# The first decode of a routed expert layer and four expert blocks, issued in a written order

## The chip, the cores and the metric

The kernel runs on one core of one Trainium2 chip. The core has a matrix engine (TensorE, PE in the profile; its weight loads are PEld), a vector engine (VectorE, DVE), an activation engine (ScalarE, ACT), GpSimd (POOL) and a queue engine that issues most transfers (SyncE, SP). The metric is the device time of one execution in microseconds; lower is better. The time before is the median of 3 runs, 2264.26 us (2261.86 to 2264.97).

## The reference, cut to what matters

Two transformer blocks on 512 tokens of width 1024, in 32-bit floats. The edit lies in the first block's expert layer:

```python
q = (xc @ w_query).reshape(c, PEER_HEADS, 2, D_HALF)
sc = jnp.einsum('chpd,hpkd->chpk', q, sub_keys)
sv, si = lax.top_k(sc, PEER_TOPK)
cand = (sv[:, :, 0, :, None] + sv[:, :, 1, None, :]).reshape(c, PEER_HEADS, PEER_TOPK * PEER_TOPK)
...
fv, fi = lax.top_k(cand, PEER_TOPK)
idx = jnp.take_along_axis(cidx, fi, axis=-1)
g = jax.nn.softmax(fv, axis=-1)
a = jax.nn.gelu(jnp.einsum('chkd,cd->chk', u_tab[idx], xc))
return jnp.einsum('chk,chkd->cd', g * a, v_tab[idx])
```

Each token has 8 heads; each head scores two sets of 128 keys, keeps 16 of each, and chooses 16 pairs. A pair names one of 128 x 128 = 16384 experts, each of which has a row in `u_tab` and a row in `v_tab`.

## The kernel before, in words

The 512 tokens are four tiles of 128. For tile 0 the chosen rows are gathered by GpSimd (`gather_steps`). For tiles 1 to 3 all 16384 experts are computed densely: for each of 128 blocks of 128 experts, the activations of 384 tokens (`h_block`) are multiplied by a gate matrix that is zero where an expert was not chosen, and then by the block's rows of `v_experts`.

A product of 32-bit numbers is made of three matmuls: a weight is loaded (`wload`, line 127, load in line 130), ScalarE makes its high half (`whi`, line 132), VectorE its low half (`wlo`, line 134), and `mm3` (lines 138 to 140) multiplies. Weight tiles have three raw buffers and four for each half. One `h_block` is such a load of 512 KB, 24 matmuls into `hps` (two buffers), and a Gelu on ScalarE (line 488) that evicts it.

Of the 128 dense blocks, 68 are computed ahead of the dense loop and stored to DRAM: `park_blocks` (line 493 is the store) is a generator, and `spread(parks, n)` emits the next n of them. These parked blocks depend on nothing but the normalised input. They are emitted at these places: one in each of the 16 steps of the routing loop, two in each of the four decodes (one ahead of each of its two halves), some in each gate group (`PARKS`), and what is left behind the last group.

The routing loop scores the keys and picks the best 16. `decode(t)` (lines 578 to 627) turns the picked places of tile t into indices and softmax gates: for each of two halves it compares, multiplies and adds 128x2048 elements on VectorE (lines 598 to 605); then come the Exp on ScalarE (line 610), three transposes on TensorE (line 622) and two copies, `sT` and `nT`. `gate_matrix(t, q, ...)` (lines 629 to 656) makes 16 tokens' part of the gate matrix: one-hot rows on VectorE and ScalarE, matmuls (line 650), an eviction (line 652), and a store to `wdr` (line 653). There are 8 groups in each of three tiles. The dense loop reads `wdr` back as `wt` (line 708) and multiplies it with the activations (line 723) before its accumulating matmuls (`acc`). A part of `wt` holds all 24 groups, so it needs the last of them.

A planner orders the instructions of each engine by their place in the text and by what is ready, within the buffers there are. Inside `with tc.manual_schedule():` each engine issues the region's instructions in the order of the text; where other instructions fall among them stays the planner's. Before the change only the dense loop stands in such a region.

Of the kernel before, what the change touches and what calls it, by code (L numbers as in the profile page):

```python
# [43 lines left out]
def body(ctx: ExitStack, tc: tile.TileContext, A: dict, out: bass.AP):  # L44
# [407 lines left out]
    with exp as st:  # L452
# [38 lines left out]
        def park_blocks():  # L491
            for k, n in enumerate(PARKED):
                SY.dma_start(park[k], h_block(n))
                yield
# [22 lines left out]
        parks = park_blocks()  # L517
        gathers = gather_steps()

        def spread(gen, n):  # L520
            for _ in range(n):
                next(gen, None)

        with mix as s1:
# [53 lines left out]
            def decode(t):  # L578
                sif = rt.tile([128, 16, 16], BF16, name="sif", bufs=2)
                V.tensor_copy(sif, si[:, t])  # L580
                fif = fi[:, t].rearrange("p h s -> p (h s)")
                over = rt.tile([128, 128], U32, name="over")
                V.tensor_scalar(over, fif, 64.0, -64.0, op0=OP.max, op1=OP.add)
                V.tensor_scalar(over, over, 2, None, op0=OP.logical_shift_right)
                V.scalar_tensor_tensor(fif, over, 12.0, fif, op0=OP.mult, op1=OP.add)
                sel = []
                for w in range(2):
                    spread(parks, 1)
                    ab = rt.tile([128, 128], U32, name=f"ab{w}")
                    if w == 0:  # L590
                        V.tensor_scalar(ab, fif, 4, None, op0=OP.logical_shift_right)
                    else:
                        V.tensor_scalar(ab, fif, 15, None, op0=OP.bitwise_and)
                    abf = rt.tile([128, 128], F32, name=f"abf{w}")
                    V.tensor_copy(abf, ab)
                    eq = rt.tile([128, 8, 16, 16], BF16, name="eq", bufs=2)
                    eqf = eq.rearrange("p h s a -> p (h s) a")
                    V.tensor_tensor(eqf, abf[:, :, None].to_broadcast([128, 128, 16]),
                                    io[:, None, 0:16].to_broadcast([128, 128, 16]), op=OP.is_equal)
                    src = sif.rearrange("p (h w) a -> p h w a", w=2)[:, :, w, None, :].to_broadcast([128, 8, 16, 16])  # L600
                    V.tensor_tensor(eq, eq, src, op=OP.mult)
                    for half in (8, 4, 2):
                        V.tensor_tensor(eqf[:, :, 0:half], eqf[:, :, 0:half], eqf[:, :, half:2 * half], op=OP.add)
                    sl_ = rt.tile([128, 128], F32, name=f"sel{w}")
                    V.tensor_tensor(sl_, eqf[:, :, 0], eqf[:, :, 1], op=OP.add)
                    sel.append(sl_)
                gw = gw0 if t == 0 else rt.tile([128, 128], F32, name="gw")
                g3 = gw.rearrange("p (h s) -> p h s", h=8)
                V.tensor_tensor(g3, fv[:, t], fv[:, t, :, 0:1].to_broadcast([128, 8, 16]), op=OP.subtract)
                SC.activation(gw, gw, AF.Exp)  # L610
                gs = sm.tile([128, 8], F32, name="gs")
                V.tensor_reduce(gs, g3, axis=AX.X, op=OP.add)
                V.reciprocal(gs, gs)
                V.tensor_tensor(g3, g3, gs[:, :, None].to_broadcast([128, 8, 16]), op=OP.mult)
                if t == 0:
                    ixf = rt.tile([128, 128], F32, name="ixf")
                    V.scalar_tensor_tensor(ixf, sel[0], 128.0, sel[1], op0=OP.mult, op1=OP.add)
                    V.tensor_copy(ix, ixf)
                    return None
                tp = psw.tile([128, 4, 128], F32, name="wps", tag="wps")  # L620
                for k, y in enumerate((sel[0], sel[1], gw)):
                    PE.transpose(tp[:, k, :], y, ident)
                sT = rt.tile([128, 3, 128], F32, name="sT", bufs=2)
                SC.activation(sT, tp[:, 0:3, :], AF.Copy)
                nT = rt.tile([128, 3, 128], F32, name="nT", bufs=2)
                SC.activation(nT, tp[:, 0:3, :], AF.Copy, scale=-1.0)
                return sT, nT
# [29 lines left out]

            quick.close()
            rw = s1.enter_context(tc.tile_pool(name="rw", bufs=2, reuse_waits="tile"))
            ahead = {1: decode(1)}  # L660
            for t in range(1, NT):
                for q in range(128 // TG):
                    if (t, q) in DECODE:
# [474 lines left out]
```

## Time and profile before

| | |
|---|---|
| median of 3 runs | 2264.26 us |
| profiled execution, its own time | 2265.66 us |
| its span, first to last instruction | 2263.9 us |
| mean granted TensorE clock | 0.995 |
| PE busy | 2213.2 us, 98% |
| DVE busy | 1518.0 us, 67% |
| ACT busy | 1012.2 us, 45% |

Busy times are of one profiled execution. A matmul that waits for an operand can count as busy, and shares over the whole span are means over stages with different limits, so the stage around the edit is read by itself. A granted clock of 1.0 is 2.4 GHz, one of 0.5 is 1.2 GHz; a figure between them is a mean over both.

### The profile page before, as it was taken

How to read it: one execution, taken by the hardware profiler on the slowest of the kernel's cores; microseconds unless marked ns; L12 is line 12 of the kernel's file. 1: busy time of each engine (PE TensorE's matmuls, PEld its weight loads, DVE VectorE, ACT ScalarE, POOL GpSimd, SP SyncE). 2: the span in 40 equal slices, each digit the busy share in tenths (PEclk: the TensorE clock that was granted, in tenths of full speed). 3: DMA queues.
4: the chain of work that ended last, by engine and by line, in shares of the span. 5: the costliest groups of instructions: out<-in, count | busy, mean ns of one | idle time of the engine just before them, and what ended most of it. 6: DMA issues, size and time to landing. Idle time of an engine off the chain costs nothing.

```text
span 2263.9 us, 30294 instructions
## 1 busy us (share of the span) xinstructions
PE 2213.2 (98%) x11337; PEld 1917.0 (85%) x11337; DVE 1518.0 (67%) x3026; ACT 1012.2 (45%) x1667; POOL 355.0 (16%) x261
## 2 busy tenths in 40 slices
PE   7999999999899999999999999999999999999998
PEld 6788878888899999888888888888866778888887
DVE  5663467899999985777777777777774667333322
ACT  5475244334996773333333333333353365222222
POOL 0000000000132422333333333333200000000000
PEclk9999999999999999999999999999999999999999
DMA  4203253443697998989989888998732124333332
GB/s 160 92 29 122 84 184 110 129 120 107 241 332 282 368 333 279 318 299 317 323 303 330 298 307 300 331 321 307 259 106 69 55 88 154 93 93 102 94 96 72
DMA packets 179875, 453.21 MB, mean 200 GB/s; under 512 B 15504, under 2 KB 84496, under 8 KB 176656
## 3 DMA queue, kind: packets, MB, share of 16 engines
q1 hardware_dynamic: 142864, 317.04, 41.7%
q0 software_dynamic: 36864, 134.23, 16.8%
q8 instruction: 89, 1.46, 0.3%
q14 instruction: 58, 0.48, 0.1%
HBM read 410.58 MB, written 40.63 MB: 199 GB/s over the span
## 4 chain that ended last, share of the span: by engine, by line
PE 83%; DVE 6%; ACT 4%; issue 4%; DMA 2%; POOL 0%; SPq 0%; DVEq 0%; ACTq 0%; POOLq 0%
PE mm L139 12%; PE mm L138 12%; PE mm L140 12%; PE acc L138 7%; PE acc L140 7%; PE acc L139 7%; PE hps L140 6%; PE hps L138 6%; PE hps L139 6%; PE wps L650 2%; ACT stg L652 1%; PE pv L372 1%; DVE wlo L134 1%; PE sc L928 1%; DVE hres L513 1%
## 5 line engine op out<-in xcount | busy, mean ns | idle before, releaser
L132 ACT ACTIVATE whi<-wraw 128x1024 fp32r<-128x1024 f32 x248 | 258.3, 1047 | 521.5 <-PE mm L139 308.2
L134 DVE TENSOR_TENSOR wlo<-wraw,whi 128x1024 fp32r<-128x1024 f32 x248 | 298.3, 1207 | 258.2 <-ACT whi L132 254.2
L138 PE MATMUL hps<-x2h,whi 128*128 128x384 f32 x1024 | 348.0, 340 | 2.1 <-ACT whi L132 1.8
L140 PE MATMUL hps<-x2h,wlo 128*128 128x384 f32 x1024 | 344.9, 337 | 1.6 <-DVE wlo L134 0.9
L139 PE MATMUL hps<-x2l,whi 128*128 128x384 f32 x1024 | 343.7, 336 | 0.0
L502 POOL DMA_INDIRECT gu<-in_u_experts_dram,ix x128 | 176.1, 1376 | 890.1 <-DVE og L644 579.6
L138 PE MATMUL acc<-whi,hh 128*128 128x512 f32 x768 | 301.8, 393 | 9.4 <-ACT hh L119 9.4
L140 PE MATMUL acc<-whi,hl 128*128 128x512 f32 x768 | 301.9, 393 | 1.1 <-DVE hl L120 1.1
L139 PE MATMUL acc<-wlo,hh 128*128 128x512 f32 x768 | 300.9, 392 | 0.0
L702 DVE TENSOR_TENSOR wlo<-wraw,whi 128x1024 fp32r<-128x1024 f32 x188 | 228.1, 1222 | 84.3 <-ACT whi L700 83.6
L700 ACT ACTIVATE whi<-wraw 128x1024 fp32r<-128x1024 f32 x188 | 196.2, 1053 | 116.0 <-issue 51.4
L511 POOL DMA_INDIRECT gv<-in_v_experts_dram,ix x128 | 177.6, 1388 | 382.2 <-DVE hres L513 263.7
L138 PEld LDWEIGHTS hps<-x2h,whi 128*128 128x128 f32 x1024 | 193.0, 189 | 5.8 <-ACT whi L132 2.1
L139 PEld LDWEIGHTS hps<-x2l,whi 128*128 128x128 f32 x1024 | 193.0, 188 | 3.0
L140 PEld LDWEIGHTS hps<-x2h,wlo 128*128 128x128 f32 x1024 | 192.7, 188 | 2.2 <-DVE wlo L134 1.1
L138 PEld LDWEIGHTS acc<-whi,hh 128*128 128x128 f32 x768 | 144.8, 189 | 42.7 <-ACT hh L119 15.0
L119 ACT ACTIVATE hh<-hw 128x384 fp32r<-128x384 f32 x128 | 67.4, 526 | 250.9 <-DVE hw L723 250.9
L140 PEld LDWEIGHTS acc<-whi,hl 128*128 128x128 f32 x768 | 144.8, 189 | 36.0 <-DVE hl L120 5.8
L139 PEld LDWEIGHTS acc<-wlo,hh 128*128 128x128 f32 x768 | 144.8, 188 | 27.6
L513 DVE SCALAR_TENSOR_TENSOR hres<-gv,ga,hres 128x1024 f32<-128x1024 f32 x128 | 164.2, 1283 | 4.6 <-DMA gv<-in_v_experts_dram,ix 3.4
L504 DVE CUSTOM_DVE_ANT_0 gu<-gu,xtok 128x1024 f32<-128x1024 f32 x128 | 154.2, 1221 | 0.0
L139 PE MATMUL mm<-x4l,whi 128*128 128x512 f32 (+1 forms) x384 | 142.4, 372 | 0.5 <-DVE x4l L120 0.5
(316 smaller groups left out, 4120.5 us busy)
## 6 DMA issues: line engine op xcount, KB each, us to landing
wraw<-in_u_cols_dram SPq DMA_DIRECT2D x128, 512.0 KB
wraw<-in_v_experts_dram SPq DMA_DIRECT2D x128, 512.0 KB
wraw<-in_w_in_dram SPq DMA_DIRECT2D x50, 512.0 KB
wdr<-stg SPq DMA_DIRECT2D x24, 1024.0 KB
wt<-wdr SPq DMA_DIRECT2D x16, 1536.0 KB
park<-hg SPq DMA_DIRECT2D x68, 192.0 KB
hg<-park SPq DMA_DIRECT2D x68, 192.0 KB
wraw<-in_w_gate_dram SPq DMA_DIRECT2D x22, 512.0 KB
```

What stands on the lines that cost most here:

```text
L119: SC.activation(hi, ps, AF.Copy)
L132: SC.activation(hi, raw, AF.Copy)
L134: V.tensor_tensor(lo, raw, f(hi), op=OP.subtract)
L138: PE.matmul(ps, lhsT=ah, rhs=bh, start=start, stop=False)
L139: PE.matmul(ps, lhsT=ah, rhs=bl, start=False, stop=False)
L140: PE.matmul(ps, lhsT=al, rhs=bh, start=False, stop=stop)
L502: GP.indirect_dma_start(out=u, out_offset=None, in_=A["u_experts"], in_offset=bass.IndirectOffsetOnAxis(ap=ix[:, s_:s_ + 1], axis=0))
L504: V.tensor_tensor_reduce(out=u, in0=u, in1=xtok, scale=1.0, scalar=0.0, op0=OP.mult, op1=OP.add, accum_out=a[:, s_:s_ + 1])
L511: GP.indirect_dma_start(out=v, out_offset=None, in_=A["v_experts"], in_offset=bass.IndirectOffsetOnAxis(ap=ix[:, s_:s_ + 1], axis=0))
L513: V.scalar_tensor_tensor(hres[:, 0, :], v, a[:, s_:s_ + 1], hres[:, 0, :], op0=OP.mult, op1=OP.add)
L700: SC.activation(hi, raw, AF.Copy)
L702: V.tensor_tensor(lo, raw, f(hi), op=OP.subtract)
```

## The change

The first decode, that of tile 1, moves into a region of written order, and two parked blocks are emitted ahead of it there. With the two that `decode` itself emits, the region holds four. The four blocks behind the last gate group become two.

```diff
             quick.close()
             rw = s1.enter_context(tc.tile_pool(name="rw", bufs=2, reuse_waits="tile"))
-            ahead = {1: decode(1)}
+            with tc.manual_schedule():
+                spread(parks, 2)
+                ahead = {1: decode(1)}
             for t in range(1, NT):
```

## Rows read from the trace of the kernel before

**Rows 1.** The page, busy time, share and instructions of each engine.

```profile
PE 2213.2 (98%) x11337; PEld 1917.0 (85%) x11337; DVE 1518.0 (67%) x3026; ACT 1012.2 (45%) x1667; POOL 355.0 (16%) x261
```

**Rows 2.** Timeline of ScalarE: start, us, line, operation, count, idle before.

```profile
535.28 0.47 ACT L488 ACTIVATE hg<-hps 128x384 f32<-128x384 f32 x1
...
539.44 0.47 ACT L488 ACTIVATE hg<-hps 128x384 f32<-128x384 f32 x1
539.93 1.28 ACT L610 ACT_TABLE_LOAD   x1
...
546.25 2.00 ACT L132 ACTIVATE whi<-wraw 128x1024 fp32r<-128x1024 f32 x2
...
551.17 0.49 ACT L488 ACTIVATE hg<-hps 128x384 f32<-128x384 f32 x1 [2.54 <-issue]
...
556.64 0.70 ACT L647 ACTIVATE og<-io,nT 128x128 f32<-128x128 f32 x2
...
572.37 0.47 ACT L488 ACTIVATE hg<-hps 128x384 f32<-128x384 f32 x1
```

**Rows 3.** Four stages: length, busy us of PE, PEld, DVE, ACT, POOL, clock, DMA.

```profile
534.00:556.60 22.60, 19.02 (x106) 17.82 (x104) 22.60 (x86) 9.88 (x14) 0.00 (x0) 0.98 0.23 73
556.60:690.00 133.40, 123.50 (x776) 119.11 (x777) 124.95 (x234) 125.29 (x251) 28.79 (x21) 0.95 0.75 271
690.00:846.30 156.30, 155.43 (x1036) 153.77 (x1036) 150.36 (x278) 116.24 (x204) 53.26 (x38) 1.00 0.91 333
846.30:878.30 32.00, 32.00 (x186) 32.00 (x185) 9.59 (x10) 10.31 (x15) 0.00 (x0) 1.00 0.89 293
```

**Rows 4.** The same table for two short stretches and the ten microseconds around their ends.

```profile
551.45:556.65 5.20, 1.59 (x6) 0.72 (x6) 5.20 (x16) 1.09 (x4) 0.00 (x0) 0.90 0.11 39
572.05:577.00 4.95, 1.76 (x11) 1.28 (x11) 3.71 (x14) 4.89 (x9) 1.15 (x2) 0.90 0.22 78
555.00:565.00 10.00, 8.42 (x39) 8.04 (x40) 9.76 (x21) 7.14 (x18) 0.00 (x0) 0.66 0.27 86
575.00:585.00 10.00, 9.15 (x46) 8.79 (x47) 8.76 (x20) 9.15 (x19) 7.18 (x5) 0.66 0.68 228
```

**Rows 5.** Timeline of TensorE at the end of the first decode.

```profile
554.24 0.63 PE L622 MATMUL wps<-ident,sel 128*128 128x128 f32 x2 [1.90 <-DVE sel L605]
...
556.64 0.69 PE L140 MATMUL hps<-x2h,wlo 128*128 128x384 f32 x1 [0.94 <-DVE wlo L134]
```

**Rows 6.** Timeline of VectorE in the first decode.

```profile
544.66 4.49 DVE L598 TENSOR_TENSOR eq<-abf,io 128x2048 bf16<-128x2048 f32 x2
...
553.80 0.69 DVE L605 TENSOR_TENSOR sel<-eq 128x128 f32<-128x128 bf16 x2
...
555.37 1.22 DVE L134 TENSOR_TENSOR wlo<-wraw,whi 128x1024 fp32r<-128x1024 f32 x1
```

**Rows 7.** Two 512 KB loads: the issue on SyncE, the ScalarE instruction that waited.

```profile
340.71 0.33 SPq L130 DMA_DIRECT2D wraw<-in_w_o_dram  x1
344.06 1.06 ACT L132 ACTIVATE whi<-wraw 128x1024 fp32r<-128x1024 f32 x1 [2.39 <-DMA wraw<-in_w_o_dram]
0.81 0.39 SPq L219 DMA_DIRECT2D xt<-in_x_dram  x1
4.87 1.06 ACT L99 ACTIVATE junk<-xt 128x1024 bf16<-128x1024 f32 x1 [1.05 <-DMA xt<-in_x_dram]
```

**Rows 8.** From the last gate group to the first accumulation: timelines of SyncE, VectorE, TensorE.

```profile
846.32 0.32 SPq L653 DMA_DIRECT2D wdr<-stg  x1
...
852.41 0.38 SPq L708 DMA_DIRECT2D wt<-wdr  x1
870.78 0.56 DVE L723 TENSOR_TENSOR hw<-hg,wt 128x384 f32<-128x384 f32 x1 [3.28 <-ACT hg L719]
871.93 0.56 DVE L120 TENSOR_TENSOR hl<-hw,hh 128x384 fp32r<-128x384 f32 x1 [0.59 <-ACT hh L119]
878.32 0.39 PE L138 MATMUL acc<-whi,hh 128*128 128x512 f32 x1
```

**Rows 9.** The table of a stretch for the matmuls and evictions of `hps` alone: PE, PEld, ACT.

```profile
846.30:878.30 32.00, 32.00 (x186) 31.87 (x184) 3.35 (x7) 1.00 0.89 293
```

## The prediction

> **What bounds the kernel now.** The page comes first [rows 1]: TensorE is recorded busy for 2213.2 us, 98% of the span, VectorE for 67%. A busy TensorE is not one at its peak, so the stage has to be looked at. The edit stands between the routing loop, whose TensorE work ends near 534 us (its last parked block is evicted at 535.28), and the loop over the experts, whose first accumulating matmul starts at 878.32 [rows 2, 8]. The table by stages [rows 3] cuts that stretch in four: the first decode (to 556.6), the gate groups while ScalarE and VectorE are both busy some 94% (to 690), the gate groups while VectorE is busy 96% (to 846.3), and a last piece of 32 us in which only TensorE is full. TensorE works on parked blocks wherever it has nothing else.
>
> Two holes show in it [rows 4]. From 551.45 to 556.65 TensorE is busy for 1.59 of 5.20 us, from 572.05 to 577.0 for 1.76 of 4.95: 6.8 us idle together, and the granted clock is 0.66 on the mean of the ten microseconds around the end of each, so part of them at the lower of the two levels. The timeline of TensorE says why [rows 5]: it waits 1.90 us for the decode's selector, then for its gate weights, and a parked block that has begun waits until 556.64 for its low half. VectorE had split that half only at 555.37, behind the whole decode [rows 6].
>
> **What the order is already.** The sixteenth block of the routing loop is evicted at 535.28; four more evictions follow from 539.44 to 551.17 [rows 2]. So four blocks already run around the decode, two about before VectorE's first large decode step at 544.66 and two within it [rows 2, 6]. Two of these belong to the first gate group: the planner pulled them forward. It also split weights far ahead: the pair of ScalarE splits at 546.25 is for blocks multiplied after 556 [rows 2]. This is possible since loads, splits, matmuls and evictions of different blocks go past one another.
>
> **The change part by part.** Nothing is added or taken away: 68 blocks, three decodes and 24 groups remain. Two blocks go from the end of the parked list (the four left after the last group become two) to the front of the decode, and every later position takes a block two numbers on. What is new is the fixed order on each engine inside the region. Call the four blocks A, B (in front), C, D (within). On SyncE's queue it reads load A, store A, load B, store B and so on; on ScalarE split A, Gelu A, split B, Gelu B, and the decode's Exp only after Gelu D; on VectorE split A, split B, head of the decode, split C, first half of the decode, split D, second half. So load B waits behind store A, which waits for Gelu A. Instructions from outside the region may still be put in between.
>
> Cost of one such link, Gelu to Gelu. An issue on SyncE takes 0.33 [rows 7], and I allow 0.4 from the end of Gelu to the next load. A 512 KB load was issued at 340.71 and released ScalarE at 344.06: 3.35 us; the first load of the kernel, 0.81 to 4.87, took 4.06 [rows 7]. I take 3.35, the DMA share being 0.11 to 0.22 in the two holes [rows 4]. The splits take 1.0 (two in 2.00 us) and 1.22 [rows 2, 6]. A block is 24 matmuls; 186 took 32.0 us, 0.172 each [rows 9], so 22 of them behind the low half are 3.8. Eviction with its start is 0.6. The sum, 0.4 + 3.35 + 1.0 + 1.22 + 3.8 + 0.6, is 10.4 us, 4.1 of them TensorE's own; three links leave 3 x 6.3 = 19 us open if nothing covers them.
>
> What covers them: blocks of later gate groups, which need neither the decode nor the region. 19 us are 4.6 blocks; the planner already keeps some five blocks in flight [rows 2], and VectorE, kept from the decode by the chain, splits their weights at once. I take 1 us lost at each link for loads that land later than planned, 3 in all (bounds 0 and 19).
>
> When does the decode end? A is evicted at 539.9 as now [rows 2]; then B at 550.3, C at 560.7, D at 571.1. VectorE's low split of C comes at 555 to 556.3. The decode's large steps run from 544.66 to 554.49 for both halves [rows 6], 4.9 us each, with small casts 5.3, to 561.6; split D ends near 566.7, the second half near 572. Exp follows Gelu D with its table load of 1.28 [rows 2]; normalisation, transposes and two copies take what they take now from the last selector step at 553.80 [rows 6] to the first gate instruction at 556.64 [rows 2], 2.8 us. With the Exp itself that is some 4.5, so the gates start at about 577: 20 us late.
>
> What the delay costs. It goes to the 24 gate groups, then the last store of the gate matrix (846.32), then the read back, issued at 852.41 when that store had landed (6.1 us), then the product with the gates, at 870.78 [rows 8]. That product waited for a Gelu, not for the read, and the first accumulating matmul waited for TensorE's blocks. The least chain is 6.1 for the store, the read of 1.5 MB (bounds 3.35, one 512 KB load, and three times that, 10.05; I take 10.05, the DMA share being 0.89 there [rows 3]), and the product and two splits of its result, three operations of about 0.56 [rows 8], 1.7: 17.9 of the 32.0 us between 846.32 and 878.32. Slack: 14 us.
>
> How much of 20 us arrives at the end? By 577 TensorE would have done (577 - 534.3) / 4.13 = 10.3 blocks after the sixteenth; before, six had been evicted by then, the last at 572.37 [rows 2]. Four blocks ahead is 4 x 1.23 = 4.9 us of VectorE that the later stretch no longer carries; the decode of token tile 0, some 11 us, may also fill VectorE's wait. So the slip is between 4 and 15 us; I take 9, about the middle, since no row says which the planner does. VectorE at 94 and 96% [rows 3] can make up little.
>
> The sum. TensorE alone: both holes gone, 6.8, and half of the clock loss (0.34 of 20 us is 6.8; bounds 0 and 6.8, since part of those stretches was paced by gate operands anyway), 3.4, less the 3 at the links: 7.2 us, so it could accumulate from 871. The gate chain: 846.3 + 9 + 17.9 = 873.2. The later of the two decides: 5 us earlier than 878.3. The expert loop behind it is written out by hand and nearly full on TensorE, so 5 us reach the end. The profiled execution took 2265.66 us (its span 2263.9 and 1.8 around it) and would take 2260.7; the median is 1.4 lower, 2264.26, and becomes 2259.
>
> **The rivals.** *The gate chain decides (slower).* Above 14 us of slip the slack is used up and each microsecond counts. With VectorE idle through the links, no filling by the other decode, and loads at 4.06, the first gate starts at 580 and all 24 us arrive: 846.3 + 24 + 17.9 = 888, 10 us later, 2274. For it: VectorE at 94 to 96% after the region. Against it: the four blocks done ahead.
>
> *The links stay open (slower).* If blocks from outside do not fill them, 19 us of idle TensorE replace 6.8, and the gates are late as well: 12 us or more, 2279 with the first rival's slip partly added. For it: it is the opposite of loading ahead. The Trainium skill, "DMA: Bandwidth & Descriptors", section "Rules for kernel authors", says to issue a transfer early, compute, and wait late, so that the fixed cost overlaps; the region's text does the contrary three times. By that page's fit (2.0 us and bytes over 436 GB/s) a 512 KB load is 3.2 us, an estimate, and the three links would be 0.5 us shorter than by my row; the trace's 3.35 and 4.06 agree with it to a microsecond. Against it: later blocks were pulled forward by five before.
>
> *Nothing moves (same).* The four blocks were about there already; what is won at 551 to 577 is given back in the ScalarE-bound groups, where fewer parked blocks are left to fill TensorE. 2264.
>
> **How the numbers follow.** Forecast 0.45; the gate chain 0.22; open links 0.10; nothing moves 0.23. What a measurement of this kernel can tell from no change is about 0.2%, 4.5 us. Faster 0.45, same 0.23, slower 0.32. The forecast's own range is 2252 (both holes and all the clock regained, no loss at the links: 13.6 less what the gate chain takes) to 2262; with the rivals 2250 to 2277.
>
> **What would show it.** Right: four parked stores, each followed by a load, 10 us apart from 540 on; the first gate operand near 577; TensorE full from 534 to 577 at clock 1.0 with blocks from outside the region between A, B, C and D; the last gate store near 855; first accumulation near 873. Wrong: holes of several microseconds in TensorE between A and D, or a last gate store after 860 with TensorE idle behind it; or a decode that ends near 556 as before, if the chain is shorter than my 10.4 us a link.

## The result, and the profile after

The changed kernel takes 2286.02 us (median of 4 runs, 2284.44 to 2287.47) against 2263.19 us of the kernel before on the same chip: a ratio of 1.0099, 95% interval 1.0086 to 1.0111, or 22.8 us slower. The forecast was 2259 us and the range ended at 2277. The profiled execution has a span of 2284.8 us, 20.9 more than before. Lines behind the edit stand two further down (the read back is L710, the product with the gates L725).

The page's busy times. The engines do the same work as before [rows 1]; TensorE has only 5.0 us more, part of it matmuls at the lower clock.

```profile
PE 2218.2 (97%) x11337; PEld 1918.9 (84%) x11337; DVE 1521.2 (67%) x3026; ACT 1011.9 (44%) x1667; POOL 358.6 (16%) x261
```

ScalarE's timeline through the region, to be laid beside [rows 2].

```profile
539.57 0.49 ACT L488 ACTIVATE hg<-hps 128x384 f32<-128x384 f32 x1 [3.67 <-PE hps L140]
...
544.19 1.06 ACT L132 ACTIVATE whi<-wraw 128x1024 fp32r<-128x1024 f32 x1 [1.53 <-DMA wraw<-in_u_cols_dram]
552.87 1.28 ACT L488 ACT_TABLE_LOAD   x1 [7.63 <-PE hps L140]
554.17 0.49 ACT L488 ACTIVATE hg<-hps 128x384 f32<-128x384 f32 x1
558.78 1.06 ACT L132 ACTIVATE whi<-wraw 128x1024 fp32r<-128x1024 f32 x1 [4.12 <-DMA wraw<-in_u_cols_dram]
567.04 0.49 ACT L488 ACTIVATE hg<-hps 128x384 f32<-128x384 f32 x1 [7.20 <-PE hps L140]
571.69 1.06 ACT L132 ACTIVATE whi<-wraw 128x1024 fp32r<-128x1024 f32 x1 [4.16 <-DMA wraw<-in_u_cols_dram]
...
580.26 0.49 ACT L488 ACTIVATE hg<-hps 128x384 f32<-128x384 f32 x1 [1.54 <-PE hps L140]
...
594.95 0.70 ACT L647 ACTIVATE og<-io,nT 128x128 f32<-128x128 f32 x2
```

Blocks A, B, C and D are evicted at 539.57, 554.17, 567.04 and 580.26: links of 14.6, 12.9 and 13.2 us, where the prediction had 10.4. The first gate operand comes at 594.95, 38.3 us later than before. SyncE's queue shows why the links are links:

```profile
540.50 0.38 SPq L130 DMA_DIRECT2D wraw<-in_u_cols_dram  x1
554.68 0.32 SPq L493 DMA_DIRECT2D park<-hg  x1
555.10 0.38 SPq L130 DMA_DIRECT2D wraw<-in_u_cols_dram  x1
567.55 0.32 SPq L493 DMA_DIRECT2D park<-hg  x1
567.97 11.28 SPq L130 DMA_DIRECT2D wraw<-in_u_cols_dram  x6
```

Each load stands behind the store of the block before. Between 540.50 and 567.97 two weight loads are issued, both of the region; no later block is loaded. TensorE's timeline, the instructions it waited for:

```profile
545.30 0.69 PE L138 MATMUL hps<-x2h,whi 128*128 128x384 f32 x1 [5.77 <-ACT whi L132]
...
559.89 0.69 PE L138 MATMUL hps<-x2h,whi 128*128 128x384 f32 x1 [7.09 <-ACT whi L132]
...
572.80 0.69 PE L138 MATMUL hps<-x2h,whi 128*128 128x384 f32 x1 [5.85 <-ACT whi L132]
```

It idles 5.77, 7.09 and 5.85 us, 18.7 in all. The first matmul behind each hole is recorded with 0.69 us, the next ones with 0.52, and the last third of the block with 0.33 to 0.34:

```profile
547.04 0.52 PE L138 MATMUL hps<-x2h,whi 128*128 128x384 f32 x1
...
551.57 0.34 PE L138 MATMUL hps<-x2h,whi 128*128 128x384 f32 x1
```

The granted clock is 0.50 from 545.30 to 551.10, from 559.90 to 564.70 and from 572.80 to 578.30, and 0.99 to 1.00 from there to the end of each block (551.30 to 552.80, 564.90 to 567.00, 578.50 to 581.00): each block began at the lower level and ended at the higher.

VectorE's timeline shows the two waits of the chain, and what it did while the decode's second half was due (575.47 onward):

```profile
559.87 1.23 DVE L134 TENSOR_TENSOR wlo<-wraw,whi 128x1024 fp32r<-128x1024 f32 x1 [9.82 <-ACT whi L132]
...
572.78 1.23 DVE L134 TENSOR_TENSOR wlo<-wraw,whi 128x1024 fp32r<-128x1024 f32 x1 [5.55 <-ACT whi L132]
...
574.33 1.23 DVE L134 TENSOR_TENSOR wlo<-wraw,whi 128x1024 fp32r<-128x1024 f32 x1
575.47 2.28 DVE L598 TENSOR_TENSOR eq<-abf,io 128x2048 bf16<-128x2048 f32 x1
577.67 1.22 DVE L134 TENSOR_TENSOR wlo<-wraw,whi 128x1024 fp32r<-128x1024 f32 x1
...
579.94 1.22 DVE L134 TENSOR_TENSOR wlo<-wraw,whi 128x1024 fp32r<-128x1024 f32 x1
...
581.68 2.29 DVE L598 TENSOR_TENSOR eq<-abf,io 128x2048 bf16<-128x2048 f32 x1
...
591.88 0.29 DVE L614 TENSOR_TENSOR gw<-gw,gs 128x128 f32<-128x128 f32 x1
```

Once the chain lets go, splits of blocks from outside and a second decode (581.68) stand between the steps of the one that the gates wait for. The four stages of [rows 3], and the last piece before the first accumulation:

```profile
534.00:556.60 22.60, 12.79 (x56) 11.63 (x55) 13.21 (x74) 5.41 (x7) 0.00 (x0) 0.85 0.17 51
556.60:690.00 133.40, 115.60 (x692) 107.89 (x693) 115.44 (x202) 108.17 (x216) 27.90 (x18) 0.95 0.67 239
690.00:846.30 156.30, 152.46 (x1019) 151.11 (x1017) 152.80 (x285) 119.92 (x217) 51.97 (x37) 1.00 0.91 330
...
867.00:900.00 33.00, 33.00 (x202) 32.86 (x201) 10.94 (x16) 13.80 (x19) 0.00 (x0) 1.00 0.79 257
```

TensorE is busy 6.2, 7.9 and 3.0 us less in the first three stages, VectorE 9.4 and 9.5 less in the first two; behind 867 TensorE is full. The end of the gates (SyncE, then TensorE), beside [rows 8]:

```profile
876.84 0.32 SPq L653 DMA_DIRECT2D wdr<-stg  x1
...
881.64 0.38 SPq L710 DMA_DIRECT2D wt<-wdr  x1
```

```profile
900.52 0.39 PE L138 MATMUL acc<-whi,hh 128*128 128x512 f32 x1
```

The matmuls and evictions of `hps` alone between these two, columns as in [rows 9]:

```profile
876.84:900.52 23.68, 23.68 (x138) 23.53 (x136) 2.38 (x5) 1.00 0.93 295
```

The last gate store comes 30.5 us later, the first accumulation 22.2 us later (900.52 against 878.32). The latter is the whole loss: what is left of the span behind it is 1384.3 us, against 1385.6 before.

### The profile page after: what moved, and what is told of

It is laid out like the page before. It is cut to its first block, busy times and chain, and to the rows that moved or that the text cites. A ratio compares the mean times of both kernels' runs of the same rounds, so it can differ in the third digit from the quotient of the medians.

```text
span 2284.8 us, 30301 instructions
## 1 busy us (share of the span) xinstructions
PE 2218.2 (97%) x11337; PEld 1918.9 (84%) x11337; DVE 1521.2 (67%) x3026; ACT 1011.9 (44%) x1667; POOL 358.6 (16%) x261
## 4 chain that ended last, share of the span: by engine, by line
PE 81%; issue 5%; DVE 5%; ACT 5%; DMA 4%; SPq 0%; POOL 0%; DVEq 0%; ACTq 0%; POOLq 0%
PE mm L139 12%; PE mm L138 12%; PE mm L140 12%; PE acc L138 6%; PE acc L140 6%; PE acc L139 6%; PE hps L140 6%; PE hps L138 6%; PE hps L139 5%; DMA wraw<-in_u_cols_dram 2%; PE wps L650 1%; PE pv L372 1%; PE sc L930 1%; DVE wlo L134 1%; ACT stg L652 1%
## 5 line engine op out<-in xcount | busy, mean ns | idle before, releaser
L138 PE MATMUL hps<-x2h,whi 128*128 128x384 f32 x1024 | 351.1, 343 | 18.7 <-ACT whi L132 18.7
L139 PE MATMUL acc<-wlo,hh 128*128 128x512 f32 x768 | 300.3, 391 | 0.0
```

What stands on the lines that cost most here:

```text
L138: PE.matmul(ps, lhsT=ah, rhs=bh, start=start, stop=False)
L139: PE.matmul(ps, lhsT=ah, rhs=bl, start=False, stop=False)
```

## The experiments

Each kernel differs from the changed one by the diff shown, unless it says otherwise. The table holds what all of them gave. "Gates late" is the start of tile 1's `nT` copy against 556.12 before; "work" is TensorE's work from 530 to 850, busy time times granted clock added up over 10 us stretches, against the 300.3 us of the kernel before (the clock is a mean over a stretch, so it is good to a few us).

| kernel | ratio (95%) | gates late | last gate store | first accumulation | its shift | work |
|---|---|---|---|---|---|---|
| before | 1 | 0 | 846.32 | 878.32 | 0 | 0 |
| after | 1.0099 (1.0086 to 1.0111) | 38.1 | 876.84 | 900.52 | +22.2 | -17.5 |
| e1_no_region | 1.0018 (1.0007 to 1.0029) | 5.2 | 860.01 | 883.69 | +5.4 | -5.1 |
| e2_two_within | 1.0073 (1.0059 to 1.0087) | 22.2 | 865.22 | 897.18 | +18.9 | -16.0 |
| e3_not_sync | 1.0090 (1.0069 to 1.0112) | 25.8 | 874.23 | 897.88 | +19.6 | -16.1 |
| e4_own_buffers | 1.0105 (1.0083 to 1.0126) | 32.9 | 877.04 | 900.73 | +22.4 | -18.8 |
| e5_warm | 1.0113 (1.0091 to 1.0135) | 36.9 | 877.14 | 900.87 | +22.6 | -19.0 |
| e6_decode_only | 1.0002 (0.9992 to 1.0012) | 16.8 | 856.69 | 880.39 | +2.1 | +0.4 |
| e7_pipelined | 1.0021 (1.0011 to 1.0031) | 15.2 | 860.84 | 884.73 | +6.4 | +0.1 |
| e8_late_gates | 1.0052 (1.0037 to 1.0068) | 15.0 | 859.57 | 891.57 | +13.3 | -12.4 |
| e9_decode_first_2 | 1.0033 (1.0022 to 1.0045) | 15.9 | 852.20 | 884.20 | +5.9 | -4.1 |
| e9_decode_first_4 | 1.0005 (0.9995 to 1.0015) | 13.6 | 852.59 | 876.26 | -2.1 | +3.2 |
| e10_later_gates | 1.0174 (1.0157 to 1.0191) | 26.9 | 882.73 | 914.73 | +36.4 | -35.1 |
| e11_ahead_and_late | 1.0139 (1.0121 to 1.0157) | 33.0 | 884.49 | 908.17 | +29.9 | -28.0 |
| e12_two_then_decode | 1.0170 (1.0153 to 1.0187) | 14.8 | 899.69 | 923.38 | +45.1 | -43.1 |
| e13_decode_then_four | 1.0214 (1.0197 to 1.0231) | 7.3 | 905.19 | 928.87 | +50.6 | -48.8 |

For e5 its 90 added matmuls (15.5 us at 0.172) are taken off the work.

**Is it the region, or the two blocks?** e1 keeps the blocks' places and takes the written order away.

```diff
-            with tc.manual_schedule():
-                spread(parks, 2)
-                ahead = {1: decode(1)}
+            spread(parks, 2)
+            ahead = {1: decode(1)}
```

> The change with the written order taken away: two parked blocks ahead of the decode, the decode after them, all left to the planner. If the written order is the whole cost (theory: the order on each engine strings the four blocks one behind the other), this is within 0.2% of the kernel before, 2259 to 2268 us, with no hole over 6 us in TensorE between 534 and 577. If moving two blocks forward in the text costs by itself (rival), it is over 2275.

1.0018: moving two blocks costs 0.2%, the written order the other 0.8%. e2 keeps the region but takes the two blocks ahead of the decode out of it (the tail has its four again):

```diff
             with tc.manual_schedule():
-                spread(parks, 2)
                 ahead = {1: decode(1)}
```

> The region holds the decode and the two blocks within it; none in front. The first of them is loaded ahead, so only one link stays open: one hole of some 6 us in TensorE near 540 and one block of 7 us behind it. The decode waits for no link before its first half and ends near 556 to 560. Theory from the four runs so far (the time follows the start of the gates, and TensorE's holes ahead of it are filled or not without much effect): 2262 to 2271. Rival (TensorE's idle time is the cost): the hole and the slow block are 9 us more, less the 3.6 us hole of before, 2268 to 2275.

1.0073. The gates were 22.2 us late, not within 4 us of before, and TensorE had two holes of 8.61 and 7.25 us, not one of 6: two blocks within the region already do most of the harm. e6 has all four blocks ahead of the region and the decode alone in it:

```diff
+            spread(parks, 4)
+            inside.append(0)
             with tc.manual_schedule():
-                spread(parks, 2)
                 ahead = {1: decode(1)}
+            inside.clear()
...
                 for w in range(2):
-                    spread(parks, 1)
+                    spread(parks, 0 if inside else 1)
```

> Four blocks in front, left to the planner; the region holds the decode alone, so no load or Gelu stands in the written order. Gates start near 556 to 561, TensorE is full to 551. If only the stringing of blocks into the decode's order costs, 2259 to 2270, as without a region; if a region around the decode costs by itself, over 2275.

1.0002. The gates came 16.8 us late, where 0 to 5 were expected, and it cost nothing. A decode alone in written order is harmless here; whole blocks in written order, one behind the other, are not.

**Which part of the order?** e3 leaves SyncE to the planner.

```diff
-            with tc.manual_schedule():
+            with tc.manual_schedule(engines={ET.PE, ET.DVE, ET.Activation}):
```

> The change with the written order on TensorE, VectorE and ScalarE only; SyncE is left to the planner, so loads may go ahead of stores. Theory: a link loses its load (some 4.2 us from Gelu to the landed weights), but split B still waits behind Gelu A on ScalarE; links of 6.5 to 9 us instead of 13 to 15, three holes of 2 to 3 us instead of 6, less time at the low clock; 2266 to 2277. If the order on SyncE is the whole cause, it is 2259 to 2268; if it is no part of it, 2282 to 2290.

1.0090: freeing SyncE's queue alone does not help. TensorE's largest holes shrank to 2.39 and 2.85 us, as expected; the time, expected at 2266 to 2277 us, did not follow. e7 starts from the kernel before and writes the region in stages: loads of blocks 16 to 20 up to three ahead, splits ahead of the matmuls that need them, the Exp behind the first block.

```diff
+            with tc.manual_schedule():
+                for k in range(16, 19):
+                    load_ahead(k)
+                split_ahead(16)
+                load_ahead(19)
+                for k in range(17, 20):
+                    split_ahead(k)
+                ahead = {1: decode(1)}
```

> A written order with the same aim, but staged: loads and splits of four blocks ahead of the decode, a fifth block loaded and split between its halves, and the Exp with the gate sums moved in front of the halves; Gelus and stores between. No link is open. TensorE should have no hole at 551 to 557, and the gates start at 555 to 559. By the gate theory it is 2256 to 2266; by the idle-time rival, 5 us of holes and low clock less than before, 2256 to 2261. Over 2270 would mean that any written order here costs.

1.0021: the same engines in a written order lose 0.2% when the order overlaps the blocks. The gates came 15.2 us late all the same, where none was expected.

**Is it the open TensorE in the links?** e4 gives the region's four blocks raw, half, PSUM and result buffers of their own.

```diff
+            own[:] = [ownp, psc]
             with tc.manual_schedule():
                 spread(parks, 2)
                 ahead = {1: decode(1)}
+            own.clear()
```

> The change, with buffers of their own (raw, high half, low half, PSUM, Gelu output) for the region's four blocks. Theory: the blocks of later gate groups did not fill the three links because the planner hands a pool's buffers out in the order of the text, so a later block cannot have one before B, C and D have theirs. Then here TensorE is full from 534 to the end of the region at clock 1.0, the links are 10 to 11 us instead of 13 to 15 since the matmuls run at the high clock, the gates still start 20 us late or more, and the time comes back to 2255 to 2272. Rival (the region holds everything later back, whatever the buffers): holes as in the change, 2282 to 2290. Rival (the late gates are what costs, not the idle TensorE): TensorE full, but still over 2280.

Now the planner fills the links. Stages of e4, columns as in [rows 3]:

```profile
534.00:600.00 66.00, 63.36 (x364) 59.91 (x362) 56.42 (x155) 33.65 (x56) 2.87 (x3) 1.00 0.38 122
600.00:700.00 100.00, 82.99 (x483) 77.36 (x484) 82.15 (x149) 89.09 (x187) 23.30 (x18) 0.85 0.73 269
```

TensorE is busy 63.36 of 66 us to 600 at full clock (57.67 before, 46.23 after), since loads of later blocks are issued between the region's. So it was the shared buffers that kept later blocks out of the changed kernel's links; that they are handed out in the order of the text was the expectation, and fits. Which of the buffers it was is not shown, since all were given at once. But the ratio stays 1.0105: the gates are still 32.9 us late, and TensorE idles from 600 to 700 instead, with 82.99 of 100 at a mean clock of 0.85. 16.2 us of that are waits for the one-hot rows that ScalarE makes for the gate groups: the blocks that filled the links have been run by then. e5 fills the links with 30 matmuls of no use behind each of the first three blocks, into a spare PSUM tile:

```diff
+                    for _ in range(30):
+                        PE.matmul(junk, lhsT=xh[:, 0, 0:128], rhs=xh[:, 0, 128:])
```

> The change with 30 extra matmuls of 128x384 behind each of the blocks A, B and C, into a PSUM tile that nobody reads: work added, none left out. They take the place of the holes and keep TensorE going. In the change a block took 7.1 to 7.5 us behind a hole, against 4.1 before. If the clock is a part of the cost, each of B, C and D takes 4.1 to 4.5 us here, the links shrink by 3 us each and the time falls by 5 to 10 us, to 2276 to 2281. If only the idle time counts, it stays at 2284 to 2290.

The clock is up (0.97 from 534 to 600, 0.84 after the change), the ratio 1.0113: a higher clock in the links wins nothing by itself. It is no test of the clock's part in the delay, since D was evicted at 576.23, 4 us earlier, and the gates came only 1.2 us earlier.

**What does a late gate cost by itself?** e8 is the kernel before with 24 chained GpSimd copies of the gate weights ahead of the transposes (added work on an idle engine); e10 has 48; e11 is e1 with 58.

```diff
+                if t == 1:
+                    z = gw
+                    for _ in range(24):
+                        z2 = rt.tile([128, 128], F32, name="late", bufs=2)
+                        GP.tensor_copy(z2, z)
+                        z = z2
+                    gw = z
```

> The kernel before, with the first tile's gate weights sent through 24 copies on GpSimd, which is idle there: the gates start later by the copies' time d (some 8 to 25 us, read from the trace), TensorE, VectorE and ScalarE are free to go on with later blocks and decodes. The prediction's slack theory: up to 14 us late costs nothing. The gate theory: the time rises by 0.7 to 1.0 of d from the first microsecond on. The idle-time rival: no rise as long as TensorE stays full to the start of the gates.

> The kernel before with 48 chained GpSimd copies of the gate weights (24 delayed the gates by 15.0 us and the first accumulation by 13.3). Late-gates theory without slack: gates start near 584.7, 28.6 us late, and the first accumulation moves by 22 to 28 us, to 900 to 906; 4 blocks stay behind the last group. Slack theory (part of the 13.3 us was lost otherwise): under 20 us.

> No written region; two blocks ahead of the decode and two less behind the last group, as in the changed kernel, and 58 chained GpSimd copies of the gate weights, which put the first gate operand near 594, where it is in the changed kernel. Late-gates theory: this delay by itself gives the whole loss: first accumulation at 898 to 906, ratio 1.008 to 1.012. If the links' open TensorE and lower clock are what costs, nothing of them is here and the loss stays under half: first accumulation before 890, ratio below 1.005.

15.0 us of delay moved the first accumulation by 13.3, 26.9 us by 36.4. e11 had the blocks' places of the changed kernel, no region, and gates 33.0 us late: +29.9, a bigger loss than the one to be explained. e10 and e11 came out above what was expected. But the three do not show lateness by itself. The transposes of the late gates stand in TensorE's queue, and TensorE waits at them for the last copy; e8, e10 and e11 in turn:

```profile
570.17 0.47 PE L629 MATMUL wps<-ident,late 128*128 128x128 f32 x1 [7.61 <-POOL late L624]
582.16 0.47 PE L629 MATMUL wps<-ident,late 128*128 128x128 f32 x1 [13.19 <-POOL late L624]
588.21 0.48 PE L629 MATMUL wps<-ident,late 128*128 128x128 f32 x1 [16.05 <-POOL late L624]
```

So each late gate opened a hole in TensorE too, against the expectation that nothing of the links' open TensorE was in e11. That the copies slowed VectorE can be left aside: its compare of 128x2048 took 2.37 us beside them and 2.29 without. And e6 (16.8 us late, 1.0002) and below e9_decode_first_4 (13.6 us late, 1.0005) have late gates, a busy TensorE, and no loss: a delay of that size is not enough.

**Is lateness necessary?** e9 has the decode alone in the region and its blocks behind it, outside: two of them (four left for the tail) or four (two left). e12 and e13 keep the four blocks inside and move the decode ahead of two or of all four.

```diff
             with tc.manual_schedule():
-                spread(parks, 2)
                 ahead = {1: decode(1)}
+                spread(parks, 4)
```

That is e13; e12 has `spread(parks, 2)` on both sides, and the e9 kernels have the last line one level out. In all four `decode(1)` emits no blocks of its own.

> The region holds the decode of tile 1 alone, none of its blocks; its two blocks come behind it in the text, so four stay behind the last group, as before the change. Late-gates theory (what counts is when the last gate store lands, plus the blocks left behind it): VectorE has the decode to itself, the gates start at 553 to 558 (before: 556.1), and the first accumulation comes within 4 us of 878.3; ratio 0.998 to 1.002. Open-TensorE theory (a written region costs by keeping blocks out of TensorE): no block may run between 536 and 555, 4 blocks or 16 us are lost, first accumulation near 894; ratio 1.007.

> The same with four blocks behind the decode in the text, so that two stay behind the last group as in the changed kernel. Late-gates theory: gates at 553 to 558; the two blocks taken from the tail give back at most 8.3 us, and they lengthen the gate groups by about as much, as they did when they were ahead of an unwritten decode: first accumulation between 872 and 884, ratio 0.998 to 1.002. Open-TensorE theory: as with two, 1.007.

> The same region with the same four blocks, written in another order: two blocks, the decode whole, two blocks. The blocks still wait on each other's stores, so links stay open; but the decode waits only for the first two. Late-gates theory: VectorE runs the decode while the second block is multiplied, the gates start at 565 to 572 instead of 594.9, the last gate store lands 12 or more us earlier than after the change (876.84), and the ratio is 1.000 to 1.005. Open-links theory (what the four serial blocks leave open on TensorE is the loss, whenever the gates start): first accumulation still at 895 or later, ratio 1.007 or more.

> The same region with the decode first and the four blocks behind it, all in written order. Late-gates theory: no block of the region holds the decode up, gates at 555 to 570, first accumulation at 876 to 886, ratio 0.999 to 1.003. Open-links theory: four serial blocks, three links, first accumulation at 895 or later, ratio 1.007 or more.

In the e9 kernels the gates came 14 to 16 us late against the forecast of none: VectorE was busy without a break from 534 to 560, with blocks' splits and another decode put ahead, so little was idle and little was lost. With e12 and e13 the late-gates theory fell. e13 has the earliest gates of any kernel with the four blocks in a region, 7.3 us late, and loses most, 1.0214. Its pair is e9_decode_first_4, which differs only in the indentation of one line: 1.0005. Two stages of e9_decode_first_4 and then of e13:

```profile
534.00:560.00 26.00, 24.14 (x140) 23.82 (x139) 26.00 (x82) 11.36 (x15) 0.00 (x0) 1.00 0.41 120
560.00:600.00 40.00, 34.90 (x212) 30.44 (x212) 36.20 (x75) 35.82 (x74) 7.70 (x7) 1.00 0.60 220
```

```profile
534.00:560.00 26.00, 1.48 (x5) 0.57 (x4) 26.00 (x96) 2.40 (x4) 0.00 (x0) 0.60 0.02 8
560.00:600.00 40.00, 27.89 (x144) 25.23 (x145) 33.75 (x65) 31.35 (x67) 12.44 (x7) 0.80 0.52 181
```

Outside the region the planner runs blocks through TensorE while VectorE decodes (24.14 of 26 us). Inside, none passes the decode: 1.48 of 26, and TensorE waits 14.16 and 9.57 us at the decode's transposes. Then they run one after the other among the gate groups. ScalarE's timeline of e13:

```profile
571.97 0.49 ACT L488 ACTIVATE hg<-hps 128x384 f32<-128x384 f32 x1 [1.77 <-PE hps L140]
...
586.60 0.49 ACT L488 ACTIVATE hg<-hps 128x384 f32<-128x384 f32 x1 [1.05 <-PE hps L140]
...
602.83 0.49 ACT L488 ACTIVATE hg<-hps 128x384 f32<-128x384 f32 x1 [1.63 <-PE hps L140]
```

Links of 14.6 and 16.2 us. The open-links theory, in turn, can't explain e4, where the links are filled; e8, e10 and e11 have no links, but a hole at their transposes.

**What holds in all sixteen.** TensorE is busy 49.4 to 50.0 of the 50 us from 800 to 850. The first accumulation follows the last gate store by 32.0 us in the five kernels with four blocks behind the last group and by 23.7 in the ten with two; the difference, 8.3, is two blocks of 24 x 0.172. e7, whose order takes five blocks instead of two, has one left and still needs 23.9: there TensorE waits 2.52 us for an eviction and its mean clock is 0.93. And the shift of the first accumulation is the work that TensorE has not done by 850, within 5 us (6.5 in e7). Whatever leaves TensorE without useful work ahead of 800 comes back in full: by a written order that nothing may overtake (e12, e13), by transposes that wait for late gates (e8, e10, e11), or by gate groups with no blocks beside them (e4). The changed kernel has 11.8 us less work done by 600, where its links stand open, and loses a further 5.8 from 600 to 800. No kernel here beats the one before; the nearest are e6 and e9_decode_first_4, the same within 0.2%.

Not settled: why e12 and e13 lose a further 24 and 20 us of work between 600 and 800, and why e10 loses more than its delay. Their traces name a part. VectorE waits in that stretch for rows that GpSimd gathers for tile 0, 10.1 us in e12, 12.0 in e13 and 7.8 in e10 against 1.0 before, and TensorE's largest hole there, in e12, waits for one-hot rows of VectorE:

```profile
761.15 3.75 PE L652 MATMUL wps<-og,oj 128*128 128x128 f32 x16 [6.80 <-DVE og L646]
```

No run takes these waits away. Nor is it settled how the changed kernel's 22.2 us divide between the open links and the late gates, since neither could be taken away without the other staying.

## Why the prediction was wrong

**The serial order was read rightly.** Store and load alternate on SyncE, the Exp of the decode follows block D, and a load takes 3.7 us to its split (540.50 to 544.19, 555.10 to 558.78, 567.97 to 571.69; 3.35 was taken). The Trainium skill's rule in "DMA: Bandwidth & Descriptors", "Rules for kernel authors", which the prediction set against the change, is borne out: waiting for a transfer right behind its issue left ScalarE idle for 4.12 and 4.16 us in the links of C and D. The 3.2 us by that page's fit in the Trainium skill, an estimate, were 0.5 short of what these loads took; the fit is given there for transfers that GpSimd issues, and these are issued by SyncE.

**The link was under-sized.** 10.4 was 13.6 on the mean. The terms that were off: the block itself, 7.1 to 7.5 us from its first matmul to the end (545.30 to 552.8, 559.89 to 567.0, 572.80 to 580.2) instead of 4.1, because TensorE came out of each hole at the lower clock and ran the larger part of the block at it; and a table load of 1.28 in the first link, since an Exp (542.34) had gone ahead of it on ScalarE.

**The step that failed: "What covers them".** "Blocks of later gate groups" were to fill the links at a loss of 1 us each, with 0 and 19 us as bounds. Nothing filled them: 18.7 us stood open, next to the upper bound of 19, in part by luck (the table load was not in that bound, and the low split, which was, ran beside TensorE's first matmuls). Three blocks that began at the lower clock came on top: 22.0 us instead of 12.4. The planner's five blocks in flight were a fact of an order in which it could hand buffers on; e4 shows that the region's blocks, taking the shared buffers in turn, shut the later ones out. This is the rival "the links stay open", given 0.10 and 2279.

**The end of the decode.** D was evicted at 580.26 instead of 571.1, 9.2 us late by the links; from there to the first gate operand were 14.7 us instead of 5.9, because outside splits and another decode came in between on VectorE. Together 18 us, so the gates were 38 late where 20 were forecast.

**The second step that failed: "Slack: 14 us".** The least chain from the last store to the first accumulation was taken for what the gates need, and the rest of [rows 8] for spare time; "the later of the two decides" made TensorE and the gate chain independent. They are not, as far as these runs go: in none of the sixteen kernels is the piece behind the last store shorter than the blocks that are left. The 17.9 us that the sum took from that store to the first accumulation were 23.7, all of it TensorE's work on blocks. In e8, 15.0 us of delay were 13.3 at the end, where the prediction would have had at most 1, though a hole at the transposes is part of them. The slip of 9 us was 30.5; the 8.3 of it that came back are the two blocks taken from the tail. The rivals, 2274 and 2279, had the direction, but 2286 lies beyond both: neither had the low clock of the three blocks, or the second decode as a delay.

**The gain of 7.2 us.** The two old holes [rows 4] did go, and larger ones took their place. e6 and e9_decode_first_4, which keep TensorE at 24.1 to 24.2 of 26 us and a clock of 0.93 and 1.00 from 534 to 560 (22.37 and 0.91 before), show that even then the end moves by +2.1 and -2.1 us only. Their gates start 14 to 17 us late; that this is what takes the gain back is not shown.

**The signals that were named.** "Holes of several microseconds between A and D" and "a last gate store after 860" were listed as signs of error; both came.

## What to carry to other kernels

A written order over whole load, compute, store sequences makes them serial, and where they share buffers with what follows it shuts that out too; ask whose buffers the covering work would use before letting it cover anything. Write order by hand for one thing alone (the decode in a region by itself cost 0 to 0.3%, and did not come earlier), or in stages that overlap (0.2%). Time between two events in a trace is slack only if the engine that is full there could do its work earlier: count what the saturated engine has still to do, and a loss ahead of the saturated stretch comes back in full.

## What had not been expected of the hardware

TensorE's granted clock was the lower of its two levels when the block behind each of the three holes (5.8 to 7.1 us) began, and rose to the higher within that block: matmuls are recorded with 0.52 us before and 0.33 to 0.34 behind the rise, and a block took 7.1 to 7.5 us instead of 4.1. The three slow blocks cost half as much again as the holes' idle time.
